# A hybrid encoder layer on one core: key rotations in batches, sums fetched first, more places for mix rows and MLP sums, the last gate's weights in quarters

## The chip, the core and the metric

The kernel runs on one core of a Trainium2 chip. TensorE (PE) multiplies matrices, VectorE (DVE), ScalarE (ACT) and GpSimd (POOL) do the elementwise work, SyncE (SP) issues nearly all DMAs between the chip's memory (DRAM) and the core's on-chip memory (SBUF). Each engine runs its own queue of instructions in order and waits on semaphores. The metric is the device time in microseconds of one execution; three executions of the kernel before gave 1338.25, 1339.09 and 1339.12 us, median 1339.09.

## The reference, cut to what matters

One layer over 1024 prompt tokens and 64 sample tokens (with 512 cached ones), model width 1024, all in float32:

```python
mod = silu(c) @ w_ada + b_ada                       # six vectors per stream
shift1, scale1, gate1, shift2, scale2, gate2 = split(mod, 6)
h = rms_norm(x, g_norm1) * (1 + scale1) + shift1
c_q, c_kv, k_rope_raw, gq, gk, gv, g_lr, g_r = split(h @ w_in)
a_out = latent attention:
    kv = rms_norm(c_kv, g_kv_lora) @ w_ukv          # 4 heads, key part 128, value 128
    k  = concat(kv key part, k_rope_raw of 64 columns)   # the rotary part is shared by the heads
    k  = rms_norm(k, g_k_head); its last 64 columns are rotated by position
    o  = chunk-causal softmax attention(q, k, v)
b_out = gated linear attention (recurrence in chunks of 64), rms_norm, * silu(g_r)
x  = x + gate1 * (concat(a_out, b_out) @ w_out)
h2 = rms_norm(x, g_norm2) * (1 + scale2) + shift2
x  = x + gate2 * (square(relu(h2 @ w_up)) @ w_down)
```

Outputs are the new x, the latents, the raw rotary keys and the state of the recurrence.

## The kernel before

Every product in float32 is made of three matmuls on parts of full precision and a remainder (`mm3`: lines L94, L95, L96), so every operand is split by ACT (the high part, L102) and DVE (the remainder, L103 and L106).

The work is written as generators, and `interleave` builds one program out of them while the kernel is traced: each `yield pe, wait, condition` says how much PE time the piece takes, how long the next piece should stay back, and what must be done before it. The first generator in the list that is ready is taken. These numbers only set the order in which instructions are written; the time of each is what the engines make of it. A tile framework adds the waits: it gives a tile of a pool with `bufs` places the place that came free longest ago, and its first writer waits for the last user of that place.

The stages that matter here, by the time in the profile:

- **Keys, values and latents (about 235 to 340 us).** `latents` makes, per tile of 128 tokens, the product `D1`: 256 latent columns and 64 columns of the raw rotary key, which ACT copies to `kraw` (L703) and SP stores. ACT squares the latent columns for their norm (L699), and scales the transposed latent into `cl` (L718). `keys_values` makes a tile's keys and values. Ahead of them it squares the tile's rotary key on ACT with the sum into column 8 of a small buffer `ssk` (L973; `ssk` has the pool's two places), and rotates it on DVE into `R` (L974 to L977) with the table `tabk`. Then, for two pairs of heads: copy of the key part `kn` on DVE (L985), its square on ACT (L987), the values (L988), the reciprocal root on POOL (L989, L991), and the scaling of `kn` (L996) and of the rotary part (L997) on DVE; PE transposes them (L1003). This is run for 13 tiles: four of cached keys, one of the sample's new keys, and eight of the prompt, most of which run later, in the attention stage (to about 425 us).
- **The early part of the output projection (about 526 to 540 us).** `out_early` fetches the first columns of the mixed rows (`mix_d`) and of the softmax sums (`rs_d`) and multiplies them (`gate`, L1267), while the last attention tiles still run.
- **The output projection (to about 650 us).** `main` goes through four column blocks. `load` fetches a block's rows in four tiles of 544 KB: `mb` (sums), `mr` (gates of the recurrence), and two `mx` (mixed rows), in the order L1438 to L1441; `mx` has two places in all, `mr` and `mb` one. DVE gates and splits them, PE multiplies, DVE adds the residual (L1478), and SP stores the row (L1480). `norm2` follows a block behind, with a small diagonal `dg` (L1507) that PE reads at L1511.
- **The MLP's first product (about 600 to 1010 us).** `weights` fetches and splits the columns of `w_up` (`ru`), and `up` makes seven products per block j by a fast scheme with sums and differences of halves. ACT copies PE's results (L1733, L1739), DVE adds (L1719) and makes the squares' sums and differences (L1754, L106) in `st` (six places) and `sc` (three places), which SP stores to `u_d` (L1695).
- **The last gate.** `last_gate` computes gate2 on DVE: `cs` (silu of the conditioning, L1817), spread over the partitions as `cb`, and for each of eight rows m one load of 512 KB (`wg5`, one place) and eight multiplications of 128x256 with sums (L1831), starting as up blocks 2 to 9 are done.

Of the kernel before, what the change touches and what calls it, by code (L numbers as in the profile page):

```python
# [10 lines left out]
F32 = mybir.dt.float32  # L11
# [8 lines left out]
P = 128  # L20
# [6 lines left out]
H = 4  # L27
# [45 lines left out]
def layer(ctx: ExitStack, tc: tile.TileContext, I, O):  # L73
# [890 lines left out]

    def keys_values(lh, ll, ki, tab, n, kv, slot, ahead=4500):
        ukh, ukl = groups["UK"]
        kn = kw.tile([P, H, P], F32, name="kn")
        ss = kw.tile([P, 9], F32, name="ssk")

        R = kw.tile([P, 1, 64], F32, name="R")  # L970
        a = kw.tile([P, 1, 64], F32, name="ra")
        t_ = kw.tile([P, 1, 64], F32, name="rt")
        ACT.activation(t_[:n, 0], kraw[:n, ki], AF.Square, accum_out=ss[:n, 8:9])  # L973
        DVE.tensor_tensor(out=a[:n, 0], in0=kraw[:n, ki], in1=tabk[:n, tab, 0], op=ALU.mult)  # L974
        DVE.tensor_tensor(out=t_[:n, 0], in0=kraw[:n, ki], in1=tabk[:n, tab, 1], op=ALU.mult)
        DVE.tensor_tensor(out=R[:n, 0, 0:32], in0=a[:n, 0, 0:32], in1=t_[:n, 0, 32:64], op=ALU.subtract)
        DVE.tensor_tensor(out=R[:n, 0, 32:64], in0=a[:n, 0, 32:64], in1=t_[:n, 0, 0:32], op=ALU.add)  # L977
        kr = kw.tile([P, 2, P], F32, name="krt", bufs=1)
        for g in range(2):
# [6 lines left out]
            for j in range(2):  # L986
                ACT.activation(kr[:n, j], pg[:, j, 0:P], AF.Square, accum_out=ss[:n, 2 * g + j:2 * g + j + 1])  # L987
# [7 lines left out]
        for g in range(2):  # L995
            DVE.tensor_tensor(out=kn[:n, 2 * g:2 * g + 2], in0=kn[:n, 2 * g:2 * g + 2], in1=rs[g], op=ALU.mult)  # L996
        DVE.tensor_tensor(out=kr[:n].rearrange("p g (e c) -> p (g e) c", e=2), in0=R[:n].broadcast_to([n, H, 64]),  # L997
                          in1=ss[:n, 4:8].rearrange("p (h o) -> p h o", o=1).broadcast_to([n, H, 64]), op=ALU.mult)
# [158 lines left out]
    def past_keys():  # L1157
        kvS.append(KV(kvA, 512))
        kvN.append(KV(kvA, 64))
        for t in (1, 2):  # L1160
            load_past(t, kw.tile([P, 2, P], F32, name="latr"))
        for t in range(4):
            yield 600, 0, has("UK")
            lh, ll = split_T(kw, past[t], 2, P, "lat")
            if t == 0:
                load_past(3, dp.tile([P, 2, P], F32, name="past", bufs=1))
            yield 0, 1000, None
            yield from keys_values(lh, ll, 8 + t, t, P, kvS[0], t, 9200)
        yield from new_keys(8)

    def new_keys(i):
# [100 lines left out]
    def out_early():  # L1272
# [142 lines left out]
    with ExitStack() as octx:  # L1415
# [127 lines left out]
    with ExitStack() as uctx:  # L1543
        def pool(name, bufs):
            return uctx.enter_context(tc.tile_pool(reuse_waits="tile", name=name, bufs=bufs))
# [264 lines left out]
        def last_gate():  # L1810

            gp = pool("gp", 1)
            yield 0, 0, has("u 2")
            cs = gp.tile([16, P], F32, name="cs")
            SP.dma_start(cs, I["vecs"][0:16])
# [5 lines left out]
                         c_d.rearrange("(o r) c -> o (r c)", o=1).broadcast_to([P, 2 * D]))  # L1821
            sums = gp.tile([P, KT, 2, 4], F32, name="sums")
            for m in range(KT):
                yield 0, 0, has(f"u {2 + m}")
                w = gp.tile([P, D], F32, name="wg5")
                SP.dma_start(w, I["w_gate2"][m * P:(m + 1) * P])
                yield 0, 6000, None
                for k in range(4):
                    ks = slice(256 * k, 256 * k + 256)
                    for s in range(2):  # L1830
                        DVE.scalar_tensor_tensor(out=ts[s][:, 0:256], in0=w[:, ks], scalar=1.0, in1=cb[:, s, ks], op0=ALU.mult,  # L1831
                                                 op1=ALU.mult, accum_out=sums[:, m, s, k:k + 1])
                    yield 0, 1000, None
            m5 = modT[:, 5]
# [211 lines left out]
```

## Time and profile before

| | |
|---|---|
| median of three executions | 1339.09 us |
| the profiled execution's own time | 1335.78 us |
| its span | 1333.7 us |
| mean granted TensorE clock | 0.999 |
| DVE busy | 913.3 us |
| ACT busy | 646.6 us |

The profile is of one execution. The span is the time from its first to its last instruction. A row of the timeline reads: start, duration, engine, line, operation, output<-inputs with shapes, count, and in brackets the idle time of that engine just ahead of it with what ended it; `SPq` is a DMA issue. A row of the waits reads: who waited <- for what, microseconds in total, times, longest. A row of the windows has the stretch, its length, busy time and count of PE, of PE's weight loads, DVE, ACT and POOL, the granted clock, the DMAs' busy share and GB/s. A row of DMA issues has the transfer, count, KB of each and the median from issue to landing.

### The profile page before, as it was taken

What the parts mean: (1) busy time and instruction counts of PE and PEld (TensorE: products, weight loads), DVE (VectorE), ACT (ScalarE), POOL (GpSimd) and SP (SyncE); (2) the same over time, 40 slices, a digit from 0 to 9 for tenths busy, and PEclk for the clock granted to TensorE, in tenths of its full rate; (3) what the DMA queues carried; (4) which work ended last, traced back from release to release, by engine and by line L of the source; (5) the groups of instructions that cost most, each with busy time, mean ns of one, the idle gap of its engine ahead of it and who ended that gap; (6) DMA issues with size and microseconds to landing.
All of it is one profiled execution on the core that took longest, in us unless ns stands there. A gap on an engine that the chain in (4) does not pass through costs nothing.

```text
span 1333.7 us, 25842 instructions
## 1 busy us (share of the span) xinstructions
PE 1307.9 (98%) x9925; PEld 1247.9 (94%) x9925; DVE 913.3 (68%) x2064; ACT 646.6 (48%) x1629; POOL 74.5 (6%) x136
## 2 busy tenths in 40 slices
PE   9999999989999999999999999999999999999999
PEld 8899999889777889999999999999999999999998
DVE  4898787455577767686998877566545955864553
ACT  5475554464366666443865444544444333443332
POOL 0100010121122200000000000000000000000000
PEclk9999999999999999999999999999999999999999
DMA  9420122374445202764345554343259755543441
GB/s 344 145 75 1 49 77 88 106 231 121 150 141 156 73 17 77 211 211 140 111 153 191 188 180 159 129 165 124 101 205 359 238 164 189 159 133 85 135 127 34
DMA packets 161198, 191.40 MB, mean 144 GB/s; under 512 B 15303, under 2 KB 112435, under 8 KB 160947
## 3 DMA queue, kind: packets, MB, share of 16 engines
q1 hardware_dynamic: 158546, 186.45, 44.3%
q10 hardware_dynamic: 2528, 3.29, 0.7%
q8 instruction: 78, 1.28, 0.4%
q14 instruction: 46, 0.37, 0.1%
HBM read 136.22 MB, written 53.49 MB: 142 GB/s over the span
## 4 chain that ended last, share of the span: by engine, by line
PE 74%; DVE 11%; DMA 7%; ACT 4%; issue 2%; POOL 1%; SPq 1%; ACTq 0%; DVEq 0%; POOLq 0%
PE mm L94 13%; PE mm L96 13%; PE mm L95 13%; PE g L94 5%; PE g L96 5%; PE g L95 5%; PE tp L94 3%; PE tp L96 3%; PE tp L95 3%; PE mm L1083 2%; PE g L886 2%; PE g L1113 1%; DMA wg<-in_w_gate 1%; DVE ts L1831 1%; PE mm L179 1%
## 5 line engine op out<-in xcount | busy, mean ns | idle before, releaser
L102 ACT CAST opers<-quad 128x512 fp32r<-128x512 f32 x112 | 69.3, 620 | 184.4 <-PE mm L96 147.2
L103 DVE TENSOR_TENSOR opers<-quad,opers 128x512 fp32r<-128x512 f32 x112 | 77.1, 689 | 114.1 <-ACT opers L102 114.1
L96 PE MATMUL mm<-opers 128*128 128x272 f32 x448 | 128.7, 288 | 0.0
L94 PE MATMUL mm<-opers 128*128 128x272 f32 x448 | 128.4, 287 | 0.3 <-DVE e L1973 0.3
L95 PE MATMUL mm<-opers 128*128 128x272 f32 x448 | 128.2, 286 | 0.0
L94 PE MATMUL mm<-ah,wh 128*128 128x272 f32 x424 | 121.8, 288 | 0.0
L96 PE MATMUL mm<-ah,wl 128*128 128x272 f32 x424 | 121.8, 288 | 0.0
L95 PE MATMUL mm<-al,wh 128*128 128x272 f32 x424 | 121.7, 287 | 0.0
L94 PE MATMUL mm<-hh,wh 128*128 128x384 f32 (+2 forms) x264 | 90.7, 344 | 0.1
L95 PE MATMUL mm<-hl,wh 128*128 128x384 f32 (+2 forms) x264 | 87.4, 331 | 0.0
L96 PE MATMUL mm<-hh,wl 128*128 128x384 f32 (+2 forms) x264 | 87.0, 330 | 0.0
L94 PEld LDWEIGHTS mm<-opers 128*128 128x128 f32 x448 | 84.6, 189 | 0.5 <-issue 0.5
L96 PEld LDWEIGHTS mm<-opers 128*128 128x128 f32 x448 | 84.2, 188 | 0.0
L95 PEld LDWEIGHTS mm<-opers 128*128 128x128 f32 x448 | 84.0, 188 | 0.0
L94 PEld LDWEIGHTS mm<-ah,wh 128*128 128x128 f32 x424 | 79.9, 188 | 0.0
L95 PEld LDWEIGHTS mm<-al,wh 128*128 128x128 f32 x424 | 79.8, 188 | 0.0
L96 PEld LDWEIGHTS mm<-ah,wl 128*128 128x128 f32 x424 | 79.6, 188 | 0.1
L103 DVE TENSOR_TENSOR opers<-ru,opers 128x544 fp32r<-128x544 f32 x108 | 77.6, 719 | 2.3 <-ACT opers L102 2.2
L102 ACT CAST opers<-ru 128x544 fp32r<-128x544 f32 x108 | 69.4, 643 | 13.3 <-PE mm L96 10.9
L102 ACT CAST wh<-ru 128x512 fp32r<-128x512 f32 x67 | 41.1, 620 | 63.9 <-PE tp L95 21.0
L94 PE MATMUL mm<-wh,hh 128*128 128x264 f32 (+3 forms) x216 | 66.4, 307 | 3.7 <-ACT cl L718 3.7
L96 PE MATMUL g<-opers 128*128 128x272 f32 x224 | 64.7, 289 | 0.0
(414 smaller groups left out, 4229.3 us busy)
## 6 DMA issues: line engine op xcount, KB each, us to landing
ru<-u_d SPq DMA_DIRECT2D x108, 272.0 KB, 2.8
raw<-in_w_ada SPq DMA_DIRECT2D x32, 512.0 KB, 4.3
ru<-in_w_up SPq DMA_DIRECT2D x32, 512.0 KB, 4.4
quad<-in_w_down SPq DMA_DIRECT2D x16, 1024.0 KB, 6.4
u_d<-st SPq DMA_DIRECT2D x60, 272.0 KB, 2.1
u_d<-sc SPq DMA_DIRECT2D x45, 272.0 KB, 2.2
raw<-in_w_in SPq DMA_DIRECT2D x22, 256.0 KB, 4.7
x<-in_xo_T SPq DMA_DIRECT2D x8, 544.0 KB, 5.2
```

The lines of the kernel that those rows point to most:

```text
L94: pin(PE.matmul(out, lhsT=ah, rhs=bh, start=first, stop=False, skip_group_check=more))
L95: pin(PE.matmul(out, lhsT=ah, rhs=bl, start=False, stop=False, skip_group_check=more))
L96: pin(PE.matmul(out, lhsT=al, rhs=bh, start=False, stop=last, skip_group_check=more))
L102: ACT.copy(hi, src)
L103: eng.tensor_tensor(out=lo, in0=src, in1=f32(hi), op=ALU.subtract)
L179: mm = PE.matmul(acc[32 * j:32 * j + 32, 0:256], lhsT=scT[:, k, :], rhs=was[k][:, 256 * j:256 * (j + 1)], start=(k == 0), stop=(k == KT - ...
L886: PE.matmul(sc[:n, a, p], lhsT=d[:, w * p + n * a:w * p + n * a + n], rhs=qv[:, :, p, a], start=True, stop=True)
L1083: PE.matmul(sp[:n, :w], lhsT=x[:, hd, :n], rhs=y[:, hd, :w], start=(j == 0), stop=(j == 4))
L1113: PE.matmul(op[:, :n], lhsT=kvs[kt // 4].v[:kw, kt % 4, hd], rhs=pt[:kw, k, :n], start=(kt == 0), stop=(kt == nkt - 1))
L1831: DVE.scalar_tensor_tensor(out=ts[s][:, 0:256], in0=w[:, ks], scalar=1.0, in1=cb[:, s, ks], op0=ALU.mult, op1=ALU.mult, accum_out=sums[:, ...
```

## The change

It has five parts. (1) `keys_values` no longer squares and rotates. A new generator `rotations` does so for four batches of tiles (the four cached ones, the sample's one, the prompt's 0 to 3 and 4 to 7) as soon as the last latent of the batch is there, in place in `kraw`, with the sums in a tile `ksum` of 13 columns. (2) `out_early` fetches the sums ahead of the mixed rows. (3) `mx` has four places and `mr` two. (4) `sc` has four places. (5) `last_gate` loads each row of its weight in four quarters of 128 KB, each with a place of its own, and fetches the next row's quarter right behind the multiplications of this one's; it starts one block later, the first four quarters are fetched ahead, and `cs` and `sums` use the places of the constants `vs` and `scT`.

```diff
+    ksum = awb.tile([P, 13], F32, name="ksum")
+
+    def rotate(k, kn, tab, n):
+
+        x, cs, sn = kraw[:n, k:k + kn], tabk[:n, tab:tab + kn, 0], tabk[:n, tab:tab + kn, 1]
+        a, t = (kw.tile([P, 4, 64], F32, name=name, bufs=1)[:n, 0:kn] for name in ("ra", "rt"))
+        ACT.activation(a, x, AF.Square)
+        DVE.reduce_sum(ksum[:n, k:k + kn], a, axis=AX.X)
+        DVE.tensor_tensor(out=a, in0=x, in1=cs, op=ALU.mult)
+        DVE.tensor_tensor(out=t, in0=x, in1=sn, op=ALU.mult)
+        DVE.tensor_tensor(out=x[:, :, 0:32], in0=a[:, :, 0:32], in1=t[:, :, 32:64], op=ALU.subtract)
+        DVE.tensor_tensor(out=x[:, :, 32:64], in0=a[:, :, 32:64], in1=t[:, :, 0:32], op=ALU.add)
+
+    def rotations():
+        for k, kn, n, last in ((8, 4, P, None), (12, 1, DEC, 8), (0, 4, P, 3), (4, 4, P, 7)):
+            yield 0, 0, has(f"lat {last}") if last is not None else None
+            yield 0, 4000 if last is not None else 0, None
+            rotate(k, kn, 0 if k == 8 else 4 if k == 12 else k, n)
...
-        ss = kw.tile([P, 9], F32, name="ssk")
-
-        R = kw.tile([P, 1, 64], F32, name="R")
...
-        ACT.activation(t_[:n, 0], kraw[:n, ki], AF.Square, accum_out=ss[:n, 8:9])
-        DVE.tensor_tensor(out=a[:n, 0], in0=kraw[:n, ki], in1=tabk[:n, tab, 0], op=ALU.mult)
-        DVE.tensor_tensor(out=t_[:n, 0], in0=kraw[:n, ki], in1=tabk[:n, tab, 1], op=ALU.mult)
-        DVE.tensor_tensor(out=R[:n, 0, 0:32], in0=a[:n, 0, 0:32], in1=t_[:n, 0, 32:64], op=ALU.subtract)
-        DVE.tensor_tensor(out=R[:n, 0, 32:64], in0=a[:n, 0, 32:64], in1=t_[:n, 0, 0:32], op=ALU.add)
+        ss = kw.tile([P, 8], F32, name="ssk")
...
-        t0, b0, t1 = fetch(mix_d, 0, 3), fetch(rs_d, 0, 3), fetch(mix_d, 4, 2)
+        b0, t0, t1 = fetch(rs_d, 0, 3), fetch(mix_d, 0, 3), fetch(mix_d, 4, 2)
...
-        interleave([weights, past_keys(), lats, query_main(), query_latents(), gates()], rest=(weights,))
+        interleave([weights, rotations(), past_keys(), lats, query_main(), query_latents(), gates()], rest=(weights,))
...
-                mx = [xw.tile([P, 4, HW], F32, name="mx") for _ in range(2)]
-                mx.append(xw.tile([P, 4, HW], F32, name="mr", bufs=1))
+                mx = [xw.tile([P, 4, HW], F32, name="mx", bufs=4) for _ in range(2)]
+                mx.append(xw.tile([P, 4, HW], F32, name="mr", bufs=2))
...
-        st2_ = pool("st2", 3)
+        st2_ = pool("st2", 4)
...
-            cs = gp.tile([16, P], F32, name="cs")
+            cs = const.tile([P, P], F32, name="cs", tag="vs")[:16]
...
-            sums = gp.tile([P, KT, 2, 4], F32, name="sums")
+            sums = const.tile([P, KT, 4, 8], F32, name="sums", tag="scT")[:, :, :, 0:2].rearrange("p m k s -> p m s k")
+            ws = {}
+
+            def load(m, k):
+                ws[m, k] = gp.tile([P, 256], F32, name=f"wg5{k}")
+                SP.dma_start(ws[m, k], I["w_gate2"][m * P:(m + 1) * P, 256 * k:256 * k + 256])
+
+            for k in range(4):
+                load(0, k)
             for m in range(KT):
-                yield 0, 0, has(f"u {2 + m}")
-                w = gp.tile([P, D], F32, name="wg5")
-                SP.dma_start(w, I["w_gate2"][m * P:(m + 1) * P])
-                yield 0, 6000, None
+                yield 0, 0, has(f"u {3 + m}")
                 for k in range(4):
-                    ks = slice(256 * k, 256 * k + 256)
+                    yield 0, 2000, None
+                    w, ks = ws.pop((m, k)), slice(256 * k, 256 * k + 256)
...
-                    yield 0, 1000, None
+                    if m + 1 < KT:
+                        load(m + 1, k)
```

The change has eleven lines more up to the MLP, so a line of before stands there eleven lines further down (L987 is L998, L1719 is L1730, L1754 is L1765).

ACT in the keys stage, where PE waits longest: first before, then with the change. `krt` is a tile's key squares, `rt` the square of the rotary key, `cn` the squares of a latent, `cl` the scaled latent.

```order
L987 ACTIVATE krt,ssk<-g 128x128 x2
L961 CAST lath<-latr 128x2x64
L987 ACTIVATE krt,ssk<-g 128x128 x2
L973 ACTIVATE rt,ssk<-kraw 64x64
L699 ACTIVATE cn,s_3437<-mm 128x256
L718 ACTIVATE cl<-mm,vT 128x128 x2
L1346 ACTIVATE sq_3460<-mm 128x320
```

```order
L998 ACTIVATE krt,ssk<-g 128x128 x2
L961 CAST lath<-latr 128x2x64
L998 ACTIVATE krt,ssk<-g 128x128 x2
L699 ACTIVATE cn,s_3438<-mm 128x256
L718 ACTIVATE cl<-mm,vT 128x128 x2
L1357 ACTIVATE sq_3461<-mm 128x320
```

The square L973 between two tiles' key squares and the latent's L699 has left this place; the batch that holds it stands elsewhere (64 rows of the sample's keys and those of four tiles at a time).

DVE at the end of the first two up blocks, before and with the change. `sc` are the tiles whose places the change adds to, `g` and `tp` PE's banks that L1719 (L1730) adds up, `wq_more` the remainder of a weight.

```order
L1754 TENSOR_TENSOR sc<-sc,st 128x544
L1719 TENSOR_TENSOR st<-st,g 128x272
L106 TENSOR_TENSOR sc<-st,sc 128x544
L1719 TENSOR_TENSOR st<-st,g 128x272
L106 TENSOR_TENSOR ru<-ru 128x512
L106 TENSOR_TENSOR st<-sc,st 128x544
L1727 SCALAR_TENSOR_TENSOR st<-st 128x544
L1719 TENSOR_TENSOR st<-st,tp 128x272
L1754 TENSOR_TENSOR sc<-sc,st 128x544
L106 TENSOR_TENSOR sc<-st 128x544
L106 TENSOR_TENSOR st<-sc,st 128x544
L106 TENSOR_TENSOR sc<-st,sc 128x544
```

```order
L1765 TENSOR_TENSOR sc<-sc,st 128x544
L1730 TENSOR_TENSOR st<-st,g 128x272
L106 TENSOR_TENSOR sc<-st,sc 128x544
L1765 TENSOR_TENSOR sc<-sc,st 128x544
L1730 TENSOR_TENSOR st<-st,g 128x272
L106 TENSOR_TENSOR st<-sc,st 128x544 x2
L106 TENSOR_TENSOR sc<-st,sc 128x544
L1738 SCALAR_TENSOR_TENSOR st<-st 128x544
L1730 TENSOR_TENSOR st<-st,tp 128x272
L106 TENSOR_TENSOR sc<-st 128x544
L1730 TENSOR_TENSOR st<-st,tp 128x272
L106 TENSOR_TENSOR ru<-ru 128x512
```

The second L1754 (the second block's) stood eight rows behind the first and stands three behind it now, and the differences that hang on it (L106 into `st` and `sc`) have come ahead of L1727 and of the L1719 of the first bank `tp`; L106 of `ru`, which the weights need, has gone from fifth to last.

DVE in the third up block, where the last gate's multiplications stand among the weights' remainders (`wl`); the numbers tell the loads apart, one number of `wg` being 512 KB before and 128 KB with the change.

```order
L103 TENSOR_TENSOR wl_7816<-tw,wh_7815 128x512
L1831 SCALAR_TENSOR_TENSOR ts_7790,sums<-wg_11741,cb 128x256
L1831 SCALAR_TENSOR_TENSOR ts_7791,sums<-wg_11741,cb 128x256
L103 TENSOR_TENSOR wl_7785<-ru,wh_7784 128x512
L1831 SCALAR_TENSOR_TENSOR ts_7790,sums<-wg_11741,cb 128x256
L1831 SCALAR_TENSOR_TENSOR ts_7791,sums<-wg_11741,cb 128x256
L1719 TENSOR_TENSOR st<-st,g 128x272
L1831 SCALAR_TENSOR_TENSOR ts_7790,sums<-wg_11741,cb 128x256
L1831 SCALAR_TENSOR_TENSOR ts_7791,sums<-wg_11741,cb 128x256
```

```order
L1848 SCALAR_TENSOR_TENSOR ts_7719,sums<-wg_11670,cb 128x256
L1848 SCALAR_TENSOR_TENSOR ts_7720,sums<-wg_11670,cb 128x256
L103 TENSOR_TENSOR wl_7745<-tw,wh_7744 128x512
L1848 SCALAR_TENSOR_TENSOR ts_7719,sums<-wg_11674,cb 128x256
L1848 SCALAR_TENSOR_TENSOR ts_7720,sums<-wg_11674,cb 128x256
L1848 SCALAR_TENSOR_TENSOR ts_7719,sums<-wg_11678,cb 128x256
L1848 SCALAR_TENSOR_TENSOR ts_7720,sums<-wg_11678,cb 128x256
L1848 SCALAR_TENSOR_TENSOR ts_7719,sums<-wg_11682,cb 128x256
L1848 SCALAR_TENSOR_TENSOR ts_7720,sums<-wg_11682,cb 128x256
L1848 SCALAR_TENSOR_TENSOR ts_7719,sums<-wg_11686,cb 128x256
L103 TENSOR_TENSOR wl_7714<-ru,wh_7713 128x512
```

Two multiplications that stood behind `wl` of `wh_7815` stand ahead of it, and seven stand ahead of the next `wl` where two stood, each pair with a load of its own. The last of the 64 now stands ahead of a `wl` that ran at 777 us in the profile of before, where the last one ran at 802 us.

More of the change, by code (lines that the diff above doesn't have):

```diff
@@ L963, in split_T, with keys_values @@
         return ch, cl
-    def keys_values(lh, ll, ki, tab, n, kv, slot, ahead=4500):
+    ksum = awb.tile([P, 13], F32, name="ksum")
[13 more added lines that the diff above has]
+            rotate(k, kn, 0 if k == 8 else 4 if k == 12 else k, n)
+    def keys_values(lh, ll, ki, n, kv, slot, ahead=4500):
         ukh, ukl = groups["UK"]
         kn = kw.tile([P, H, P], F32, name="kn")
-        ss = kw.tile([P, 9], F32, name="ssk")
-        R = kw.tile([P, 1, 64], F32, name="R")
-        a = kw.tile([P, 1, 64], F32, name="ra")
-        t_ = kw.tile([P, 1, 64], F32, name="rt")
-        ACT.activation(t_[:n, 0], kraw[:n, ki], AF.Square, accum_out=ss[:n, 8:9])
-        DVE.tensor_tensor(out=a[:n, 0], in0=kraw[:n, ki], in1=tabk[:n, tab, 0], op=ALU.mult)
-        DVE.tensor_tensor(out=t_[:n, 0], in0=kraw[:n, ki], in1=tabk[:n, tab, 1], op=ALU.mult)
-        DVE.tensor_tensor(out=R[:n, 0, 0:32], in0=a[:n, 0, 0:32], in1=t_[:n, 0, 32:64], op=ALU.subtract)
-        DVE.tensor_tensor(out=R[:n, 0, 32:64], in0=a[:n, 0, 32:64], in1=t_[:n, 0, 0:32], op=ALU.add)
+        ss = kw.tile([P, 8], F32, name="ssk")
         kr = kw.tile([P, 2, P], F32, name="krt", bufs=1)
@@ L988, in keys_values @@
             DVE.tensor_copy(kv.v[:n, slot, 2 * g:2 * g + 2], pg[:, :, P:2 * P])
-            POOL.tensor_scalar(out=ss[:n, 4 + 2 * g:6 + 2 * g], in0=ss[:n, 2 * g:2 * g + 2], scalar1=ss[:n, 8:9],
+            POOL.tensor_scalar(out=ss[:n, 4 + 2 * g:6 + 2 * g], in0=ss[:n, 2 * g:2 * g + 2], scalar1=ksum[:n, ki:ki + 1],
                                scalar2=192 * EPS, op0=ALU.add, op1=ALU.add)
@@ L996, in keys_values @@
             DVE.tensor_tensor(out=kn[:n, 2 * g:2 * g + 2], in0=kn[:n, 2 * g:2 * g + 2], in1=rs[g], op=ALU.mult)
-        DVE.tensor_tensor(out=kr[:n].rearrange("p g (e c) -> p (g e) c", e=2), in0=R[:n].broadcast_to([n, H, 64]),
+        DVE.tensor_tensor(out=kr[:n].rearrange("p g (e c) -> p (g e) c", e=2), in0=kraw[:n, ki:ki + 1].broadcast_to([n, H, 64]),
                           in1=ss[:n, 4:8].rearrange("p (h o) -> p h o", o=1).broadcast_to([n, H, 64]), op=ALU.mult)
@@ L1167, in past_keys @@
             yield 0, 1000, None
-            yield from keys_values(lh, ll, 8 + t, t, P, kvS[0], t, 9200)
+            yield from keys_values(lh, ll, 8 + t, P, kvS[0], t, 9200)
         yield from new_keys(8)
@@ L1178, in new_keys @@
         if i == 8:
-            yield from keys_values(lh, ll, 12, 4, n, kvN[0], 0, 4200)
+            yield from keys_values(lh, ll, 12, n, kvN[0], 0, 4200)
         else:
-            yield from keys_values(lh, ll, i, i, n, kvs[i // 4], i % 4)
+            yield from keys_values(lh, ll, i, n, kvs[i // 4], i % 4)
         done.add(f"k {i}")
@@ L1821, in last_gate @@
                          c_d.rearrange("(o r) c -> o (r c)", o=1).broadcast_to([P, 2 * D]))
-            sums = gp.tile([P, KT, 2, 4], F32, name="sums")
+            sums = const.tile([P, KT, 4, 8], F32, name="sums", tag="scT")[:, :, :, 0:2].rearrange("p m k s -> p m s k")
[5 more added lines that the diff above has]
+                load(0, k)
             for m in range(KT):
-                yield 0, 0, has(f"u {2 + m}")
-                w = gp.tile([P, D], F32, name="wg5")
-                SP.dma_start(w, I["w_gate2"][m * P:(m + 1) * P])
-                yield 0, 6000, None
+                yield 0, 0, has(f"u {3 + m}")
                 for k in range(4):
-                    ks = slice(256 * k, 256 * k + 256)
+                    yield 0, 2000, None
+                    w, ks = ws.pop((m, k)), slice(256 * k, 256 * k + 256)
                     for s in range(2):
-                        DVE.scalar_tensor_tensor(out=ts[s][:, 0:256], in0=w[:, ks], scalar=1.0, in1=cb[:, s, ks], op0=ALU.mult,
+                        DVE.scalar_tensor_tensor(out=ts[s][:, 0:256], in0=w, scalar=1.0, in1=cb[:, s, ks], op0=ALU.mult,
                                                  op1=ALU.mult, accum_out=sums[:, m, s, k:k + 1])
-                    yield 0, 1000, None
+                    if m + 1 < KT:
+                        load(m + 1, k)
             m5 = modT[:, 5]
```

## The prediction

> **What bounds the kernel now.** I read the page's table of busy times first, then TensorE's table of waits, then the timeline around the longest of them.
>
> ```profile
> PE 1307.9 (98%) x9925; PEld 1247.9 (94%) x9925; DVE 913.3 (68%) x2064; ACT 646.6 (48%) x1629; POOL 74.5 (6%) x136
> PE mm L94 <- ACT cl L718: 3.7, 1, 3.7
> PE tp L1123 <- ACT prob L1094: 2.5, 3, 1.5
> PE g L94 <- DVE st L1719: 1.6, 3, 1.0
> PE tp L1511 <- DVE dg L1507: 1.5, 1, 1.5
> PE mm L96 <- DVE wq_more L103: 1.1, 1, 1.1
> PE tp L94 <- DVE st L1719: 0.9, 1, 0.9
> PE mm L94 <- ACT st L1733: 0.7, 1, 0.7
> ```
>
> TensorE (PE) is busy for 98% of its span of 1333.7 us. The change neither adds nor removes a matmul, and its order on PE stays. So it can move the time in two ways only: PE's waits, some 25 us in all, and the clock. The rows above (total, times, longest) are the waits that the change can reach.
>
> **Part 1: rotations in batches (keys).** The longest wait, on ScalarE (ACT), VectorE (DVE) and PE:
>
> ```profile
> 296.45 0.27 ACT L987 ACTIVATE krt<-g 128x128 f32<-128x128 f32 x1
> 299.01 0.26 ACT L973 ACTIVATE rt<-kraw 64x64 f32<-64x64 f32 x1 [2.20 <-DVE krt L997]
> 299.27 0.36 ACT L699 ACTIVATE cn<-mm 128x256 f32<-128x256 f32 x1
> 299.63 0.60 ACT L718 ACTIVATE cl<-mm,vT 128x128 f32<-128x128 f32 x2
> 300.28 0.42 PE L94 MATMUL mm<-wh,hh 128*128 128x320 f32 x1 [3.67 <-ACT cl L718]
> 300.00:302.00 2.00, 1.72 (x10) 1.72 (x11) 1.49 (x4) 0.76 (x3) 0.55 (x2) 0.89 0.27 70
> 302.00:304.00 2.00, 2.00 (x10) 2.00 (x9) 0.07 (x1) 0.00 (x0) 0.00 (x0) 0.50 0.36 114
> 304.00:306.00 2.00, 2.00 (x12) 1.99 (x12) 0.00 (x0) 0.34 (x2) 0.00 (x0) 0.76 0.15 54
> ```
>
> PE waits for `cl`, whose two copies stand on ACT behind L699, and that behind L973, the square of one tile's rotary key. L973 waited 2.20 us for DVE's L997 of the tile before (it needs the small buffer of sums). L973 is gone here. L699 then follows L987 at 296.72; from L699's start to the end of `cl` it is still 0.96 us (299.27 to 300.23), so `cl` ends at 297.68 and PE goes on at 297.72 instead of 300.28: **−2.56 us**. Late next is L987 itself, which nothing in the change moves here.
>
> After this wait the granted clock falls: 0.89, 0.50 and 0.76 in the three windows of 2 us above, with 10 matmuls where full speed gives 16. The share missing from 1 (0.11 + 0.50 + 0.24) times 2 us is **−1.7 us** if the drop goes. From 0.50 as the floor the drop lasted some 3.4 us. The waits of 1.5 us show none (the window of the second is in part 3), and 1.1 us is shorter than these; so I take it as gone.
>
> [...]
>
> The 13 squares and 52 small DVE operations become 4 and 20, and the wide ones have to go somewhere:
>
> ```profile
> 269.57 0.42 DVE L996 TENSOR_TENSOR kn<-kn,ssk 128x256 f32<-128x256 f32 x1 [0.47 <-POOL ssk L991]
> 269.62 0.86 PE L1003 MATMUL tp<-ident,kn 128*128 128x128 f32 x4
> ```
>
> The first batch stands ahead of the second copy of `kn` (L985), three microseconds before: five operations of up to 256 columns, about 0.35 us apart, for the narrow ones. It delays that copy by some 0.7 us, and through ACT and GpSimd the second L996; the 0.47 us that DVE waits there is GpSimd's, and about 0.4 us of the delay is taken up on the way. PE's transposes L1003 read it at once: **+0.3 us** (0 to 0.7). The later batches come where PE's own matmuls run ahead of the keys; I cost them at nothing; the upper 0.4 us of the bound is for a cover that isn't there.
>
> **Part 2: the sums' fetch first.**
>
> ```profile
> 526.12 0.37 SPq L1280 DMA_DIRECT2D raw<-mix_d  x1
> 527.98 0.37 SPq L1280 DMA_DIRECT2D raw<-rs_d  x1
> 532.78 1.01 DVE L1267 TENSOR_TENSOR raw<-raw 128x816 f32<-128x816 f32 x1 [1.45 <-DMA raw<-rs_d]
> 536.26 0.66 PE L1123 MATMUL tp<-ident,prob 128*128 128x128 f32 x4 [1.48 <-ACT prob L1094]
> raw<-mix_d SPq DMA_DIRECT2D x1, 408.0 KB, 4.0
> ```
>
> The gate L1267 waits for the sums, issued 1.86 us after the rows and landed at 532.75, 4.8 us after issue; the rows took 4.0. Behind the gate on DVE stand the maxima from which ACT makes `prob`, for which PE waits 1.48 us. With the two issues exchanged the sums land at 526.12 + 4.8 = 530.9 and the rows at 527.98 + 4.0 = 532.0: the gate starts 0.8 us earlier, **−0.8 us** (−0.1 to −1.2). Then the rows are late.
>
> **Part 3: four places for mix rows, two for the gate's rows.**
>
> ```profile
> 562.15 2.42 SPq L1480 DMA_DIRECT2D x_d<-x  x4
> 567.89 0.52 SPq L1439 DMA_DIRECT2D mr<-r_d  x1
> 569.50 0.46 SPq L1440 DMA_DIRECT2D mx<-mix_d  x1
> 575.99 1.29 DVE L1267 TENSOR_TENSOR mx<-mx,mb 128x1088 f32<-128x1088 f32 x1 [3.13 <-DMA mx<-mix_d]
> 580.00:600.00 20.00, 18.54 (x146) 18.20 (x146) 17.20 (x42) 9.76 (x20) 1.23 (x2) 1.00 0.52 163
> ```
>
> DVE stood for 3.13 us for `mx` and then worked without a break up to `dg`, which PE missed for 1.46 us. The fetch of `mx` is issued only 0.4 us earlier now, since it stands behind a store of x2 that waits for DVE; but `mr` (544 KB), which no longer waits for its place, leaves SP right behind the four stores that end at 564.57, 3.3 us earlier, and moves while the queue has room. Its share at the rate of those microseconds (about 1.5 us) comes off too: `mx` lands about 1.9 us earlier. An L1478 now waits behind the gate; its bank is not needed soon. `dg` comes 1.5 to 2 us earlier: **−1.4 us** (−0.4 to −1.5).
>
> **Part 4: a fourth place for an up block's sums.**
>
> ```profile
> 690.69 1.57 SPq L1695 DMA_DIRECT2D u_d<-st  x2
> 693.60 0.72 DVE L106 TENSOR_TENSOR st<-sc,st 128x544 f32<-128x544 f32 x1 [0.25 <-DMA u_d<-st]
> 697.47 0.73 DVE L106 TENSOR_TENSOR sc<-st 128x544 f32<-128x544 f32 x1 [1.23 <-DMA u_d<-sc]
> 702.95 0.39 PE L96 MATMUL mm<-ah,wq_more 128*128 128x272 f32 x1 [1.06 <-DVE wq_more L103]
> ```
>
> DVE waits for a store out of one of three places, while PE later misses it twice (0.86 + 1.06). With four, the wait of 1.23 goes, and what stood behind it moves up. But an operation that stood later now comes first and needs the second of the two stores of `st`. The first was issued at 690.69 and held DVE to 693.60, 2.9 us later; the second, issued 1.2 us after it, would by that land at 694.8, where DVE arrives at about 694.1: some 0.75 us come back. DVE is otherwise full up to 703, so PE goes on near 702.0 instead of 702.95: **−1.0 us** (−0.8 to −1.9).
>
> **Part 5: the last gate by quarters.**
>
> ```profile
> 758.43 0.43 DVE L1719 TENSOR_TENSOR st<-st,g 128x272 f32<-128x272 f32 x1
> 784.22 0.43 DVE L1831 SCALAR_TENSOR_TENSOR ts<-wg,cb 128x256 f32<-128x256 f32 x1 [1.87 <-DMA wg<-in_w_gate]
> 798.82 0.43 DVE L1831 SCALAR_TENSOR_TENSOR ts<-wg,cb 128x256 f32<-128x256 f32 x1 [2.56 <-DMA wg<-in_w_gate]
>   DVE ts L1831: 14.5, 7
> lat_d<-cl SPq DMA_DIRECT2D x3, 128.0 KB, 2.2
> DMA to landing us min/median/max: 3.8/3.9/4.4
> 643.26 1.28 ACT L1817 ACT_TABLE_LOAD   x1
> ```
>
> DVE stands 14.5 us for the eight loads of 512 KB (3.9 us each), its other work queued behind. The adds L1719 behind such waits, the one at 758.43 and two after 798.82, are what PE misses (`g` L94, 1.6 us in three waits), and behind 784.22, through ACT, the L1733 (0.7). In the changed order all 64 multiplications stand before about 778 us, so the waits behind 784.22 and 798.82 go for certain; the question is 727 to 778, where they stand closer and 28 reloads of 128 KB each follow the multiplication that frees the place. No such load is in this trace; nearest are the 128 KB of `lat_d` (2.2 us) below and the 512 KB (4.4 us at most) above. I take 2.3, `lat_d`'s 2.2 and 0.1 to the issue. By hand, with DVE's rows 0.35 us (256 and 272 columns), 0.6 (512) and 0.64 (544) apart as they follow each other there, the add of 758.43 then starts near 755.9, and PE loses nothing: **−2.4 us** (the 1.6 and the 0.7, before rounding). With 4.0 us it starts near 760.7 and PE loses 2.75 us where it lost 0.4: +0.4 in all. SP's 24 more issues stand behind DVE's work that also precedes the stores and loads after them, so they add no wait of their own. The Silu moves to about 238 us, with a table load of 1.28 us each way; the exponentials behind it come 1.2 us later, but what reads them on PE's path runs near 245: nothing.
>
> [...]
>
> **Sum.** −2.56 − 1.7 + 0.3 − 0.8 − 1.4 − 1.0 − 2.4 = **−9.6 us** against the profiled run of 1335.78 us. The median of the three runs is 1339.09; I take the difference over to it: **1329.5 us**.
>
> **Rivals.** The row is DVE's fullest window ahead of part 4's place.
>
> ```profile
> 670.00:680.00 10.00, 10.00 (x81) 9.95 (x80) 9.87 (x20) 9.37 (x24) 0.00 (x0) 1.00 0.08 29
> ```
>
> - *The clock.* The drop stays, after a shorter wait or elsewhere, or is missing from the timed runs already: −7.9, **1331.2**. For it: it was seen once, in one execution.
> - *Quarter loads at 4 us.* Part 5 gives +0.4: −6.8, **1332.3**. For it: the same stretch carries 512 KB loads and stores.
> - *DVE eats what came before.* DVE is full there (9.87 of 10 us). If it can't start that stretch earlier, parts 1 to 3 (6.2 us) turn into waits there, and −3.4 is left: **1335.7**. Against it: the stretch begins with the second norm, which waits for PE's matmuls, and PE had no wait in it.
> - *The other side: quarter loads chain.* Each place's reload, its landing and the next multiplication form a chain on DVE between 727 and 778. From 2.3 to 4.0 us PE lost 2.75 us plus slack, beyond that about 2.7 us for each us of landing; at 6.5 us all is lost, and at 7.5 the kernel is slower by 2.7: **1342**. Against it: 4.4 us is the longest load of four times the size there.
> - *It doesn't do what it says:* the waits return one step on (another DMA, another queue), within 2.7 us of before: about **1338**.
>
> **How the numbers follow.** A measurement of this kernel can tell about 0.2% (2.7 us) from no change. Forecast 0.55 (its own range 1327.8 to 1331); clock 0.12; loads at 4 us 0.13; DVE eats 0.09; chain 0.05; returned 0.06. Half of the "eats" case goes to no change, since its number lies close to 1336.4. Faster 0.85, same 0.10, slower 0.05. The range takes in the low ends of all terms (−11.3, so 1327.8, and 0.8 for the short waits of PE that I haven't counted) and the three rivals up to 1335.7: 1327.0 to 1336.0.
>
> **What would show it.** Right: PE's wait for `cl` at about 1.1 us and a clock of 1.00 from 296 to 306; no PE wait for L1507's `dg`; `prob` below 0.8 us; L1831's successor done before 780 with short DVE waits. Wrong: a second clock drop, DVE waits for the quarter loads over 1.5 us each near 750 to 775 with PE's L94 behind L1719, or a new PE wait above 1 us in 640 to 700.

## The result and the profile after

The changed kernel took 1329.53 us (median of 6 runs, 1327.36 to 1330.71), the kernel before 1338.94 us beside it (6 runs, 1337.22 to 1340.09): a ratio of 0.9939, with a 95% interval of 0.9927 to 0.9952 (the two medians alone give 0.9930). That is 1329.5 us, the time that was predicted. The profile shows that the terms behind it were not all right.

The profiled execution of the changed kernel took 1329.64 us, with a span of 1327.8 us, 5.9 us shorter than the span before. TensorE is as busy as it was (1308.0 against 1307.9 us), so what was gained lies in its waits. The table of TensorE's waits after the change (who waited <- for what: us in total, times, longest):

```profile
PE tp L1014 <- DVE kn L1007: 2.6, 4, 0.9
PE tp L1134 <- ACT prob L1105: 2.2, 3, 1.2
PE tp L1522 <- DVE dg L1518: 1.6, 1, 1.6
...
PE mm L94 <- ACT cl L718: 0.8, 1, 0.8
...
PE mm L96 <- DVE wq_more L103: 0.7, 1, 0.7
```

The wait for `cl` fell from 3.7 to 0.8, the wait at `wq_more` from 1.1 to 0.7, and the three waits of `g` L94 for L1719 (now L1730) and the one for L1733, 2.3 us together, are gone. `prob` and `dg` stand where they stood. New are two of the waits for the scaled key part `kn`. The timeline of TensorE has them, and the one that `dg` ends:

```profile
270.42 0.44 PE L1014 MATMUL tp<-ident,kn 128*128 128x128 f32 x2 [0.56 <-DVE kn L1007]
329.05 0.33 PE L1014 MATMUL tp<-ident,kn 64*128 64x64 f32 x2 [0.60 <-DVE kn L1007]
532.98 0.66 PE L1134 MATMUL tp<-ident,prob 128*128 128x128 f32 x4 [1.22 <-ACT prob L1105]
575.83 0.71 PE L1511 MATMUL tp<-ones,acc 128*128 128x1 f32 x6 [0.30 <-DVE acc L1497]
581.35 1.00 PE L1522 MATMUL tp<-dg,ones 128*128 128x128 f32 x6 [1.59 <-DVE dg L1518]
```

ScalarE where TensorE waited longest, from the timeline of the changed kernel:

```profile
296.34 0.27 ACT L998 ACTIVATE krt<-g 128x128 f32<-128x128 f32 x1
296.50 0.20 ACT L998 ACTIVATION_READ_ACCUMULATOR krt<-g 128x1 f32 x1
296.59 0.39 ACT L699 ACTIVATE cn<-mm 128x256 f32<-128x256 f32 x1
296.86 0.21 ACT L699 ACTIVATION_READ_ACCUMULATOR cn<-mm 128x1 f32 x1
296.95 0.64 ACT L718 ACTIVATE cl<-mm,vT 128x128 f32<-128x128 f32 x2
```

Nothing stands between L998 and L699 any more, as the prediction had it. Last, the granted clock, in windows of 3.41 us laid out from the first clock record of the run (columns: stretch, length, busy time and count of PE, its weight loads, DVE, ACT and POOL, granted clock, DMA share, GB/s):

```profile
579.86:583.27 3.41, 1.93 (x14) 1.81 (x15) 2.10 (x10) 0.88 (x3) 1.23 (x2) 1.00 0.95 270
583.27:586.69 3.42, 3.42 (x18) 3.42 (x17) 3.42 (x10) 2.84 (x6) 0.00 (x0) 0.50 0.93 306
586.69:590.10 3.41, 3.41 (x29) 3.41 (x29) 3.29 (x6) 3.34 (x7) 0.00 (x0) 1.00 0.13 42
```

The drop at 302 us is gone, and one of the same length stands at 583, right behind the wait for `dg`: 18 matmuls in it, 29 in the next window.

Span against span, the changed kernel's waits sum up so: `cl` -2.9, the waits at 270 and 329 +0.6 and +0.7 (0.09 of it in a second short one), `prob` -0.3, the norm (1.59 + 0.30 against 1.46) +0.4, `wq_more` and its neighbour -1.25, the last gate -2.4, clock 0, and 0.8 of start-up waits of the profile before that the change doesn't touch: -5.9 us.

### The profile page after: what moved, and what is told of

Same layout as the page of the kernel before. It is cut to its first block, busy times and chain, and to the rows that moved or that the text cites. A ratio compares the mean times of both kernels' runs of the same rounds, so it can differ in the third digit from the quotient of the medians.

```text
span 1327.8 us, 25836 instructions
## 1 busy us (share of the span) xinstructions
PE 1308.0 (99%) x9925; PEld 1248.3 (94%) x9925; DVE 911.6 (69%) x2032; ACT 645.5 (49%) x1608; POOL 75.1 (6%) x136
## 4 chain that ended last, share of the span: by engine, by line
PE 75%; DVE 11%; DMA 6%; ACT 4%; issue 2%; POOL 1%; SPq 1%; DVEq 0%; ACTq 0%; POOLq 0%
PE mm L94 13%; PE mm L96 13%; PE mm L95 13%; PE g L94 5%; PE g L96 5%; PE g L95 5%; PE tp L94 3%; PE tp L96 3%; PE tp L95 3%; PE mm L1094 2%; PE g L886 2%; PE g L1124 2%; PE mm L179 1%; DMA x<-in_xo_T 1%; DMA mx<-mix_d 1%
## 5 line engine op out<-in xcount | busy, mean ns | idle before, releaser
L103 DVE TENSOR_TENSOR opers<-quad,opers 128x512 fp32r<-128x512 f32 x112 | 77.2, 690 | 114.5 <-ACT opers L102 114.5
L94 PE MATMUL mm<-opers 128*128 128x272 f32 x448 | 128.4, 287 | 0.3 <-DVE e L1991 0.3
L94 PE MATMUL mm<-ah,wh 128*128 128x272 f32 x424 | 121.8, 288 | 0.0
L94 PE MATMUL mm<-hh,wh 128*128 128x384 f32 (+2 forms) x264 | 90.7, 344 | 0.1
L94 PEld LDWEIGHTS mm<-opers 128*128 128x128 f32 x448 | 84.5, 189 | 0.5 <-issue 0.5
L94 PEld LDWEIGHTS mm<-ah,wh 128*128 128x128 f32 x424 | 79.9, 188 | 0.0
L103 DVE TENSOR_TENSOR opers<-ru,opers 128x544 fp32r<-128x544 f32 x108 | 77.7, 719 | 2.9 <-ACT opers L102 2.7
L94 PE MATMUL mm<-wh,hh 128*128 128x264 f32 (+3 forms) x216 | 65.7, 304 | 0.8 <-ACT cl L718 0.8
```

The lines of the kernel that those rows point to most:

```text
L94: pin(PE.matmul(out, lhsT=ah, rhs=bh, start=first, stop=False, skip_group_check=more))
L103: eng.tensor_tensor(out=lo, in0=src, in1=f32(hi), op=ALU.subtract)
```

## The experiments

Each kernel is compared with the kernel before on the same chip. Lines of the kernels differ by a few; a row's tiles say which operation it is.

**Part 1 alone** (`rotations`, `ksum`, nothing else of the change).

> Part 1 alone in the kernel before (rotations in four batches, parts 2 to 5 left as before). By the waits: PE's wait for cl near 296 us falls from 3.67 to about 0.8 (-2.9), a new wait of about 0.5 near 270 and about 0.6 near 328; the clock's drop leaves 302 us and is either gone (-1.7) or comes back behind the wait of 1.5 for dg near 580. In all -1.8 to -3.5 against before. Rival (the profile of before was an untypical execution, and the timed runs hold something that the change removes elsewhere): more than -4.5.

1334.26 us, ratio 0.9977 (0.9965 to 0.9989), so some 3.1 us. The wait for `cl` was 1.34, those at 270 and 329 were there (0.56 and 0.58). The drop at 302 was gone, and one came at 582.56 behind a `dg` wait of 1.84. Part 1 does what was claimed at its place and brings the two small waits by itself.

**Own columns for the sums alone**: the squares stay where they were, but their sums go to a place of their own.

```diff
+    ksum = awb.tile([P, 13], F32, name="ksum")
...
-        ss = kw.tile([P, 9], F32, name="ssk")
+        ss = kw.tile([P, 8], F32, name="ssk")
...
-        ACT.activation(t_[:n, 0], kraw[:n, ki], AF.Square, accum_out=ss[:n, 8:9])
+        ACT.activation(t_[:n, 0], kraw[:n, ki], AF.Square, accum_out=ksum[:n, ki:ki + 1])
...
```

> Only the sums of the 13 rotary squares go to a tile of their own, in the kernel before; squares and rotations stay tile by tile. If the wait near 296 us comes from the shared small buffer of sums: PE's wait for cl falls below 1.2 us here too, and no wait comes near 270; -2.5 to -4.5 in all. Rival (the squares' number and place on ACT cost it, so batches are needed): the wait for cl stays above 2.5 us and the time within 1 us of before.

1337.95 us, ratio 1.0006 (0.9991 to 1.002): nothing, and the wait stayed at 3.61. Its timelines of ScalarE and of VectorE say why:

```profile
299.92 0.26 ACT L975 ACTIVATE rt<-kraw 128x64 f32<-128x64 f32 x1 [2.45 <-DVE R L979]
300.18 0.36 ACT L699 ACTIVATE cn<-mm 128x256 f32<-128x256 f32 x1
```

```profile
298.81 0.42 DVE L998 TENSOR_TENSOR kn<-kn,ssk 128x256 f32<-128x256 f32 x1 [0.65 <-POOL ssk L993]
299.15 0.42 DVE L999 TENSOR_TENSOR krt<-R,ssk 128x256 f32<-128x256 f32 x1
299.61 0.18 DVE L978 TENSOR_TENSOR R<-ra,rt 64x32 f32<-64x32 f32 x1
299.71 0.18 DVE L979 TENSOR_TENSOR R<-ra,rt 64x32 f32<-64x32 f32 x1
```

The square (L973 of before, L975 here, where the one that waits is the next tile's, of 128 rows) has a second tie: it writes into the scratch `rt`, and the last reader of that scratch (L979) stands on VectorE behind the same scaling (L998, L999) that GpSimd holds up. With the first tie cut the second ends the wait at the same time. The sums' buffer alone was not the cause; it takes the square out of that place in ScalarE's queue, as part 1 does.

**Parts 4 and 5 alone.**

> Parts 4 and 5 alone (fourth place for sc, last gate by quarters). By the waits: -1.25 near 700 us and -2.5 between 758 and 804, so -3.7 us; nothing changes before 640 us apart from the Silu near 238. Rival (DVE's full stretch or the loads of quarters give it back later): -2 or less.

1333.3 us, ratio 0.9974 (0.9961 to 0.9988), 3.5 us; the sum had 3.4 for the two. Only a wait of 0.38 was left of those in the MLP. The wait for `cl` was 3.65 as before, and here two windows in a row ran at half speed, the first from 298.88, while TensorE still stood:

```profile
295.47:298.88 3.41, 1.32 (x8) 1.00 (x6) 2.30 (x7) 0.81 (x5) 2.12 (x4) 1.00 0.07 22
298.88:302.30 3.42, 1.86 (x7) 1.86 (x8) 2.28 (x8) 1.75 (x8) 0.74 (x2) 0.50 0.26 72
302.30:305.71 3.41, 3.41 (x15) 3.41 (x14) 0.00 (x0) 0.00 (x0) 0.00 (x0) 0.50 0.30 99
305.71:309.12 3.41, 3.41 (x25) 3.29 (x25) 1.03 (x3) 1.93 (x6) 0.74 (x2) 1.00 0.08 22
```

A wait of nearly the same length (3.67 us there, 3.65 here) was thus followed by one window at half speed in the profile of before and by two here, where the edges of the windows are others (298.14 us there, 298.88 here).

**The change without part 3** (two places for `mx`, one for `mr`).

> The changed kernel with two places for mx and one for mr as before. Theory (the fourth place lets the gate move ahead of an L1489 on DVE; its store, and behind that store on SP the fetch of x, are late by as much): the wait of 0.3 near 575 goes, dg is waited for 1.3 to 1.5 us, the time is 0.2 to 0.6 us under the changed kernel. Rival (the places help, as predicted): dg is waited for over 2.5 us or the time is 1 us or more above the changed kernel.

1330.15 us, ratio 0.9949 (0.9932 to 0.9966), within its interval of the change's. The `dg` wait was 1.95 and the 0.30 was not there: 1.95 against 1.89, so part 3 shifts the wait more than it shortens it. Neither case came as it was stated (1.3 to 1.5 us, or over 2.5). What it shifts shows in the queues. VectorE and SP in the changed kernel, then SP without part 3:

```profile
572.39 1.29 DVE L1278 TENSOR_TENSOR mx<-mx,mb 128x1088 f32<-128x1088 f32 x1 [2.31 <-DMA mx<-mix_d]
573.60 0.49 DVE L1489 SCALAR_TENSOR_TENSOR x<-mm,modT,x 128x272 f32<-128x272 f32 x1
574.01 1.28 DVE L1278 TENSOR_TENSOR mx<-mx,mr 128x1088 f32<-128x1088 f32 x1
...
578.79 1.16 DVE L1489 SCALAR_TENSOR_TENSOR x<-mm,modT,x 128x208 f32<-128x208 f32 x4 [0.71 <-DMA x<-in_xo_T]
...
580.94 0.46 DVE L1518 TENSOR_SCALAR dg<-ident,st 128x128 f32<-128x128 f32 x2
```

```profile
574.12 0.34 SPq L1491 DMA_DIRECT2D x_d<-x  x1
574.51 1.03 SPq L1458 DMA_DIRECT2D x<-in_xo_T  x2
```

```profile
571.14 0.32 SPq L1491 DMA_DIRECT2D x_d<-x  x1
571.52 1.06 SPq L1458 DMA_DIRECT2D x<-in_xo_T  x2
```

With part 3 one L1489 stands behind the gate instead of ahead of it. Its store leaves SP later, and the fetch of the next `x` behind it 3 us later (574.51 against 571.52). The gate is 1.46 us earlier than without part 3 (572.39 against 573.85), but `x` is late, VectorE waits 0.71 us for it in front of `dg`, and `dg` is only 0.53 us earlier (580.94 against 581.47).

**The change with `x` fetched one block ahead.**

```diff
-                load_x(c)
+                if w == 0:
+                    load_x(c)
                 if w + 1 < 4:
+                    load_x(WORDER[w + 1])
                     load(WORDER[w + 1])
```

> The changed kernel, with the four fetches of x in the middle stage issued one block ahead (before the fetch of the next block's mix rows; the first block's stays where it is). Theory A (part 3 failed because the store of the block's result, and the fetch of x queued behind it on SP, now stand behind the gate's wait for mix rows): the vector engine's wait for x near 578.8 (0.71) goes, TensorE's wait for dg near 580 falls from 1.59 to under 0.8, the clock drop at 583 (3.41 us at half speed) goes, and the time falls by 1.5 to 3 us against the changed kernel, to 1326.5 to 1328. Theory B (the wait hangs on the mix rows that land 6 us after their issue, not on x): the dg wait stays over 1.3 us, the drop stays, the time is within 1 us of 1329.5.

1326.5 us, ratio 0.9927 (0.9914 to 0.9941). TensorE has no wait over 0.15 us between 540 and 690 us, and no drop. One of its windows there, at the full clock:

```profile
582.00:584.00 2.00, 2.00 (x18) 2.00 (x17) 2.00 (x6) 2.00 (x6) 0.00 (x0) 1.00 0.88 269
```

And VectorE in it, whose gate is not earlier than in the changed kernel (573.60 against 572.39):

```profile
573.60 1.29 DVE L1278 TENSOR_TENSOR mx<-mx,mb 128x1088 f32<-128x1088 f32 x1 [2.12 <-DMA mx<-mix_d]
...
578.63 0.77 DVE L1520 TENSOR_SCALAR dg<-ident,st 128x128 f32<-128x128 f32 x3 [0.76 <-POOL st L1517]
...
579.86 1.27 DVE L1278 TENSOR_TENSOR mx<-mx,mr 128x1088 f32<-128x1088 f32 x1
```

So `dg` did not need an earlier gate. But two things differ in front of it, and not one. VectorE's wait of 0.71 us for `x` is gone, and its order is another: the second gate (L1278 with `mr`) and the second of the two remainders L103 stand behind `dg` here, and ahead of it in the changed kernel. `dg` starts 2.31 us earlier (578.63 against 580.94), so the wait is the smaller part of it and the order the larger; no run has the one without the other. In the kernel without part 3 both operations also stand ahead of `dg`, VectorE did not wait for `x` there, and `dg` was still waited for 1.95 us.

**The same, and the sample's batch of rotations later** (released by "lat 2" instead of "lat 8", the sample's own latent, which is made first; its sums run on VectorE at 271.39 us in place of 266.12).

> The kernel with x fetched ahead, and the sample's batch of rotations released after the wait for "lat 2" instead of "lat 8". Theory A: the new waits of TensorE at 269.9 (0.56) and 328.4 (0.60) come from the batch that stands ahead of key work on the vector engine: the first goes, and with it 0.5 us or so, to 1326 to 1327.5. Theory B: the wait at 270 hangs on the eviction chain before it and not on the batch: it stays at 0.5 or more, and the time is that of the kernel with x ahead alone within 0.5 us. For both the wait for cl near 297 must stay under 1.5.

1326.71 us, ratio 0.993 (0.9917 to 0.9942). The wait at 270 fell to 0.20, as theory A has it; the time did not move, as theory B has it. In its profile TensorE waits 0.74 at 328.6 and 1.43 at 532.1, where the kernel with `x` ahead alone had 0.33 and 1.07 in this profile and 0.93 and 1.32 in its second one (below). These two waits differ by as much between profiles of one kernel as the wait that went, so where its 0.5 us stayed is open.

**The change with three places for `sc` again** (part 4 undone).

> The changed kernel with three places for an up block's sums again. If the prediction's part 4 is right by itself, the waits near 700 come back from 0.67 to between 1.5 and 2 us (0.86 and 1.06 before) and the time is 0.8 to 1.3 us above the changed kernel. Rival: the quarter loads of part 5 had freed the vector engine and the queue there as well, so the waits stay under 1 us and the time does not move.

1330.88 us, ratio 0.9954 (0.994 to 0.9967). The waits near 700 came back at 0.67, 1.06 and, at 757, 0.48, so 1.5 us more than with four places, and the time is 2 us above that of the next kernel on the same chip. So part 4 is right by itself, and worth a little more than the prediction had; the intervals of the two ratios overlap, so it is the trace and not the time that shows it. A longer wait for `kn` near 330 in this profile (1.33 us, 0.60 in the changed kernel's) may be part of the 2 us.

**The change with the mix rows ahead of the sums again** (part 2 undone).

> The changed kernel with the mix rows fetched ahead of the sums' rows again. Theory A (part 2 worth what the trace of after shows, 0.26 us): the wait near 531.8 is 1.3 to 1.6 us and the time within 0.5 us of the changed kernel, which this many rounds can't tell from no change. Theory B (the prediction's 0.8 us): the wait is 1.9 or more and the time 0.6 to 1 us higher.

1328.92 us, ratio 0.9944 (0.9932 to 0.9956). The wait for `prob` was 1.23, against 1.22 with the sums first, which is below both cases' figures. VectorE's gate, first in the changed kernel, then with the rows first:

```profile
529.50 1.01 DVE L1278 TENSOR_TENSOR raw<-raw 128x816 f32<-128x816 f32 x1 [1.19 <-DMA raw<-mix_d]
```

```profile
529.32 1.01 DVE L1278 TENSOR_TENSOR raw<-raw 128x816 f32<-128x816 f32 x1 [1.21 <-DMA raw<-rs_d]
```

SP issued the later of the two fetches at these times, first in the changed kernel (with the fetch behind it in one row), then with the rows first:

```profile
525.00 2.98 SPq L1291 DMA_DIRECT2D raw<-mix_d  x2
```

```profile
524.64 0.37 SPq L1291 DMA_DIRECT2D raw<-rs_d  x1
```

The gate starts 4.5 and 4.7 us behind the later issue, whichever of the two that is. Part 2 is worth nothing.

**Three kernels on one chip**: the changed kernel again, the one with `x` ahead again, and `x` ahead without part 3.

> The changed kernel once more, unaltered, beside the next two on one chip, for its time there and for the clock. [...] Theory B (a wait over 1.5 us always brings the drop): all runs list 0.999 or less. Time 1329.5 within 1.5 us.

> The kernel with x fetched one block ahead once more, beside the changed kernel on the same chip. Theory A: no wait for dg over 0.5 us, the clock at 1.0 in most runs, and 2 to 3.5 us less than the changed kernel. Theory B (the 3 us between the two were of chip and day): within 1 us of it.

> x fetched one block ahead, and the places for mix rows and the gate's rows as before the change (part 3 undone). Theory A (the late x, not the late mix rows, set the wait for dg): the wait for dg stays below 0.6 us without part 3, and the time is within 1 us of the kernel with x ahead. Theory B (both are needed, since the gate then waits for its rows as before): the gate's wait for mx is 3 us again, the wait for dg comes back to 1 to 1.5 us, and the time is 1 to 3 us above the kernel with x ahead.

They took 1329.06 (1326.77 to 1329.64; ratio 0.9934, 0.9922 to 0.9946), 1327.13 (1326.56 to 1327.66; 0.9922, 0.991 to 0.9935) and 1326.53 us (1325.15 to 1330.04; 0.9921, 0.9908 to 0.9935). Fetching `x` ahead is 1.9 us better than the change, a little less than expected, and the intervals of the ratios overlap; that the wait and the drop are gone is shown in both profiles of it. Without part 3 it is as good: the wait for `dg` is gone there too, with the second gate behind `dg` on VectorE as well. So with `x` fetched early part 3 isn't needed. That the late `x` alone set the wait, as theory A has it, is not shown, since the order on VectorE changed with the fetch both times.

For the clock, the changed kernel's second profile has two windows of nearly the same idleness, one with a drop behind it and one without:

```profile
296.60:300.02 3.42, 1.90 (x13) 1.64 (x12) 1.89 (x7) 1.83 (x9) 2.67 (x5) 1.00 0.18 49
300.02:303.43 3.41, 3.41 (x25) 3.37 (x24) 1.33 (x3) 1.36 (x6) 0.49 (x2) 1.00 0.41 129
579.91:583.32 3.41, 1.90 (x13) 1.78 (x14) 2.10 (x10) 0.91 (x3) 1.23 (x2) 1.00 0.83 228
583.32:586.74 3.42, 3.42 (x18) 3.42 (x17) 3.42 (x10) 2.81 (x6) 0.00 (x0) 0.50 1.01 326
```

The wait for `cl` was 1.52 in it, with the whole key chain some 0.75 us later than in the first profile, so that wait varies from execution to execution. Four of its five runs list a clock of 1.0 and one, the profiled one, 0.999, so theory B, which had 0.999 or less in all of them, falls. How long the wait was in the other four was not recorded.

## Why the prediction was right, and where it was not

The mechanism for the sign and for most of the size is shown: the change shortens TensorE's waits, and the parts that do it are 1 and, together, 4 and 5 (3.1 and 3.5 us alone). The sum of 9.6 us, however, was made against one profiled execution, and there the change brought 6.1 us (1335.78 to 1329.64). The last step, that the distance of 3.3 us from the profiled run to the median carries over, failed: after the change that distance is gone (1329.64 and 1329.53). The two errors cancelled, so that the number came out to the tenth was luck. Of the prediction's own signs, the wait for `cl` came as it should, `prob` below 0.8 and no wait for `dg` did not, and one of the signs of being wrong, a second drop of the clock, did.

- **Part 1, the wait for `cl`: right**, -2.9 us where -2.56 was predicted (0.76 left in place of 1.1), though it varies (1.34 and 1.52 in other profiles). The cause given for L973's wait, the small buffer of sums, was only one of two ties; the experiment on it shows the scratch as the other. Since L973 goes altogether, the number was not touched by that.
- **The new wait at 270: right in place, larger in size**, 0.56 against 0.3. The *sample's* batch stands ahead of the second copy of `kn`, not the cached tiles' alone. Missed was the place at 328, another 0.7: TensorE reaches it earlier than before, while the keys there hang on a store (`cq_d`) for which VectorE waits 1.66 us, to 324.00. "I cost them at nothing" was wrong for a stage whose other engine doesn't move up with TensorE.
- **The clock: wrong in the profile, more than right in the median.** In the profile the drop came back at 583, behind the `dg` wait, so that term was 0. What waits of this length do to the clock was misjudged: "The waits of 1.5 us show none" is true of the kernel before, where windows with 1.94 and 1.95 us busy of 3.41 had none behind them, but in the changed kernel one with 1.93 us busy had. Over many runs the clock did rise. Of 50 runs of the kernel before that were timed beside the experiments (one more took 2560.51 us and is left out), 31 list a granted clock of 0.998 or less (median 1338.5 us) and 19 list 0.999 or 1.0 (1335.9); the profiled one, 0.999 and 1335.78, was of the second group. With the old rotations (own sums alone, parts 4 and 5 alone) 18 of 24 runs list 0.998 or less, with the new ones 3 of 60, one of them the 0.949 of the last section. By the 3.41 us at half speed in the profiles, a window is 0.0013 of the run; by that estimate most runs of before lost two windows or more and not one. This fits the 3.3 us between profile and median that the change closed; the six runs behind the median of before list no clock, so for them it is not shown.
- **Part 2: wrong**, nothing in place of -0.8 (the 0.26 in the profile is there without the part). The step that failed is "the rows at 527.98 + 4.0 = 532.0": a row's time of 4.0 us was that of the fetch issued first. The one issued last is there 4.5 to 4.7 us later, whichever it is, so the order of the two made no difference.
- **Part 3: wrong**, next to nothing (1.89 us of waits against 1.95 without it) in place of -1.4. The gate was earlier, as predicted. The step that failed is "An L1478 now waits behind the gate; its bank is not needed soon": what matters behind it is not its bank but its store, with the fetch of `x` behind that store on SP. The prediction had asked what is queued behind on VectorE and not followed it over to SP. Nor did it look at what else stands ahead of `dg` on VectorE. With `x` ahead the wait went, with and without part 3, and there the second gate stands behind `dg`; how much is the landing of `x` and how much this order stays open.
- **Part 4: right**, -1.25 in place of -1.0, and 1.5 us of waits come back when it is undone.
- **Part 5: right in its sum**, -2.4 as predicted, **by too low a landing time.** The quarters take longer than the 2.3 us that were chosen, as the view of the issuing line in the changed kernel shows (who waited for it, times; then from issue to landing):

```profile
  DVE ts L1848: 4.6, 5
...
DMA to landing us min/median/max: 2.2/3.5/4.8
```

  VectorE waited for them five times, 4.6 us in all in place of 14.5, and the last multiplication ended at 773.4, before the predicted 778. The price put on longer landings ("With 4.0 us it starts near 760.7 and PE loses 2.75 us") was too high: at a median of 3.5 TensorE lost nothing here. The chain is a real risk in single executions, though. The second profile of the kernel with `x` ahead, VectorE and then TensorE:

```profile
745.93 0.42 DVE L1850 SCALAR_TENSOR_TENSOR ts<-wg,cb 128x256 f32<-128x256 f32 x1 [3.17 <-DMA wg<-in_w_gate]
...
751.64 0.43 DVE L1732 TENSOR_TENSOR st<-st,g 128x272 f32<-128x272 f32 x1
```

```profile
752.13 0.39 PE L94 MATMUL g<-ah,wh 128*128 128x272 f32 x1 [1.22 <-DVE st L1732]
```

Of the rivals, "the clock" described the profile (a drop elsewhere) and not the median; "DVE eats what came before" did not show: part 1 alone keeps its 3.1 us to the end, and the waits near 700 are 0.75 and 1.06 there, as without it. Why the wait for `cl` varies between 0.6 and 1.5 from one execution to the next was not tried. Part 5 was not undone alone, so its share is read from the traces.

## What to carry to other kernels

When a change lets an operation go ahead of another in an engine's queue, follow what the other one *issues*: its store, and whatever stands behind that store on the DMA queue; here a fetch left 3 us late, and VectorE's wait of 0.71 us for it took much of the 1.46 us by which the gate had moved up. And when such an edit takes a wait away, compare the order of the engine's queue before the cause is named: here the fetch and the order changed together. Swapping two fetches that one operation needs gave nothing here, since it waited for the later one: it started 4.5 us behind the later issue in one order and 4.7 in the other. A profile is one execution: before a sum is shifted to the median, look whether the listed runs share its clock, since in one profile here, of two stretches that were equally idle (1.90 us busy of 3.41), one had a window at half speed behind it and the other none.

## What the runs showed of the hardware

The granted clock fell to 0.50 for 3.413 us (the length in both traces' clock records) in the kernel before (from 301.55) and in the changed kernel (from 583.27), and with parts 4 and 5 alone for twice as long (298.88 to 305.71). Counted from the first clock record, which comes 4.59 us after the start in the profile of before and 6.42 us after it in the changed kernel's, the drop begins after 87.0 such lengths in the one and after 169.0 in the other. In the 3.41 us just ahead of a drop TensorE was busy for 1.27 us (the kernel before), 1.32 (parts 4 and 5 alone), 1.57 (part 1 alone), 1.88 (three places for `sc`), 1.90 (the changed kernel again) and 1.93 us (the changed kernel). No drop stood behind windows that were busy for 1.88, 1.94 and 1.95 us (the kernel before), 1.90 (the changed kernel again) and 2.12 us (three places for `sc`). So near 1.9 us the busy time did not tell the two apart here (it is partly modelled, so a sharp edge would look blurred). The kernel before:

```profile
294.73:298.14 3.41, 1.88 (x12) 1.56 (x10) 1.72 (x5) 1.39 (x9) 2.11 (x4) 1.00 0.12 40
298.14:301.55 3.41, 1.27 (x8) 1.27 (x9) 2.33 (x9) 1.75 (x8) 0.74 (x2) 1.00 0.21 51
301.55:304.97 3.42, 3.42 (x15) 3.42 (x14) 0.52 (x2) 0.00 (x0) 0.00 (x0) 0.50 0.41 127
```

One wait of 3.67 us is split over two windows here: the first, 1.88 us busy, had no drop behind it, the second, 1.27 us busy, had one. One run of the kernel with `x` ahead lists a clock of 0.949 and was no slower (1326.93 us) than its neighbours; what that record holds was not settled.
